# A second buffer for one activation tile in a block of mLSTM, S5 and expert lookup on one Trainium2 core

## The chip, the cores and the metric

The kernel runs on one core of one Trainium2 chip. The metric is the device time of one execution in microseconds (us). Before the change it is 3209.36 us, the median of three runs (3203.93 to 3209.98). A separate execution was recorded by the hardware profiler; every row below comes from that one.

The engines are named as in the profile: PE multiplies matrices (PEld loads its weights), DVE and ACT work on tiles in on-chip memory, POOL and SP here mostly issue DMAs (SPq is SP's DMA queue). Sixteen DMA engines serve all queues.

## What is computed

The reference is one block on 512 tokens of width 2048: a normalisation, a projection, a chunked mLSTM and an S5 scan, an output projection with a residual, and then the part that matters here, a lookup of experts. Each token and each of 8 heads picks 16 of 16384 experts; the activation of an expert is a GELU of the token's dot product with a row of the first table `u_tab`, and it weighs a row of the second table `v_tab`:

```python
def block(args):
    xt, it, gt = args
    ue = jnp.take(u_tab, it, axis=0)
    ve = jnp.take(v_tab, it, axis=0)
    act = jax.nn.gelu(jnp.einsum('td,ted->te', xt, ue).astype(f32), approximate=False)
    return jnp.einsum('te,ted->td', (gt * act).astype(ve.dtype), ve)
```

## The kernel before

The experts are taken in two ways. 72 groups of 128 experts (28 fixed ones, 44 chosen at run time) are computed densely for all 512 tokens; the picks that fall outside these groups, called rare, are gathered row by row.

**The first table's stage** is the loop `for n, (i, q) in enumerate(units)`: 72 groups `i`, each in four quarters `q`, so 288 units. A unit transposes four blocks of the table tile `ur` on PE (L1485), splits them into a high part `uh` on ACT (L1487) and a low part `ul` on DVE (L1495), and makes 12 matmuls of 512 columns (L116 to L118, in the helper `mm3`) into one accumulator. `h_step` issues `u_unit` (the transposes and `uh`) three units ahead and `u_low` (the `ul`) two ahead of the matmuls. After a group's fourth quarter ACT writes the GELU of the accumulator into a tile `hg` (L1507) and SP stores it to `hg_d` (L1508). `hg` has one buffer, so the next group's L1507 waits until this store has landed. `ur` is loaded by SP for the fixed groups and gathered by POOL for the chosen ones (L1053 in `gather`), two groups ahead.

**Beside it** a generator is advanced after each unit, as far as a budget of 3 per unit goes. `gbuild` makes the table of gates: eight chunks of 64 tokens, each built in a tile `Gb` of one buffer. DVE makes one-hot tiles (L1071, L1450), PE multiplies them into a bank `tp` (L1438, three such banks), ACT writes the bank into `Gb` (L1439), and when a chunk is full SP stores it with four DMAs of 1 MB to `gt_d` (L1459) in pieces of 64 numbers. The first L1439 of the next chunk writes into the same tile, so it waits for all four. After a chunk, `HOLD` keeps the table of gates back for eight units:

```python
            for a in range(0, P, 32):
                sp.dma_start(gv[:, a:a + 32, c:c + GC], Gb[:, a:a + 32, :])
            UT["hold"] = UT["step"] + HOLD
```

In these units the budget goes to `rare`: POOL gathers 128 rows of a table into a tile `gr` (L1349, 1 MB, three buffers in this stage), and DVE multiplies and sums each (`junk`, L1346). All stores on SP's queue are issued in the order of the program, so an `hg` store that follows a chunk's four stores goes behind them.

**Memory.** Tiles on the right side of the on-chip memory are `pk` (kept to the end), then `ix` (closed after `flags`), and on it the pools of the stages. `tri` and `oneb` are constants in `pk`; their last readers are matmuls in `select` and `flags`.

After this stage the second table's stage multiplies all groups with `v_tab` in two halves and finishes the rare picks.

Of the kernel before, what the change touches and what calls it, by code (L numbers as in the profile page):

```python
# [8 lines left out]
F32 = mybir.dt.float32  # L9
# [3 lines left out]
BF16 = mybir.dt.bfloat16  # L13
# [6 lines left out]
P = 128  # L20
T = 512
# [27 lines left out]
def hybrid_block(ctx: ExitStack, tc: tile.TileContext, x, norm1_g, w_in, b_gates, conv_w, mnorm_g,  # L49
# [7 lines left out]
    def pool(name, bufs, side="left"):  # L57
        return tc.tile_pool(name=name, bufs=bufs, side=side, reuse_waits="tile")
# [32 lines left out]
    def mm_bank(shape=(P, 512)):  # L91
        return PS["p"].tile(list(shape), F32, name="mm", bufs=PS["mm"])
# [22 lines left out]
    def mm3(o, ah, al, bh, bl, start, stop):  # L115
        pe.matmul(o, ah, bh, start=start, stop=False)  # L116
        pe.matmul(o, ah, bl, start=False, stop=False)  # L117
        pe.matmul(o, al, bh, start=False, stop=stop)  # L118
# [738 lines left out]
    pk = ctx.enter_context(pool(name="pk", bufs=1, side="right"))  # L857
    iotaF = pk.tile([P, P], F32, name="iotaF")
    pcol = pk.tile([P, 1], F32, name="pcol")
    jt = pk.tile([P, P, 2], BF16, name="jt")  # L860
    tri = pk.tile([P, P], BF16, name="tri")
    oneb = pk.tile([P, P], BF16, name="oneb")
    i1b = pk.tile([P, T], BF16, name="i1b")
    i2b = pk.tile([P, T], BF16, name="i2b")
    DT = pk.tile([P, 5, T], BF16, name="DT")
# [7 lines left out]
    ix = ixs.enter_context(pool(name="ix", bufs=1, side="right"))  # L873
    i1T, i2T, gT = (ix.tile([P, T], F32, name=n) for n in ("i1T", "i2T", "gT"))
    subT = ix.tile([P, 2, P], F32, name="subT")

    xn_d = dram.tile([T, D], F32, name="xn_d")
    gt_d = dram.tile([P * P, T], F32, name="gt_d")
# [586 lines left out]
    up = ustk.enter_context(pool(name="up", bufs=1))  # L1465
# [32 lines left out]
    def h_unit(i, q):  # L1498
        if q == 0:
            UT["h", i] = mm_bank()  # L1500
        uh, ul = UT.pop(("u", i, q))
        for a in range(4):
            k = q * 4 + a
            mm3(UT["h", i], uh[:, a, :], ul[:, a, :], xh[:, k, :], xl[:, k, :], k == 0, k == 15)
        if q == 3:
            hg = up.tile([P, T], F32, name="hg")
            s.activation(hg, UT.pop(("h", i)), AF.Gelu)  # L1507
            sp.dma_start(hg_d[i], hg)  # L1508

# [3 lines left out]
    def h_step(i, q):  # L1513
        n = i * 4 + q
        while un[0] < len(units) and un[0] < n + 4:
            u_unit(*units[un[0]])
            un[0] += 1
        while un[1] < len(units) and un[1] < n + 3:
            u_low(*units[un[1]])
            un[1] += 1  # L1520
        h_unit(i, q)
# [197 lines left out]
```

## Time and profile before

| | |
|---|---|
| median of three runs | 3209.36 us |
| the profiled execution, its own time | 3199.87 us |
| its span | 3198.1 us |
| PE, PEld busy | 91%, 77% |
| DVE, ACT, POOL busy | 70%, 31%, 26% |
| mean granted clock of TensorE | 0.956 of full speed |
| DMA | 691.93 MB, 216 GB/s over the span |

Busy time of PE counts overlapping matmuls and is no measure of how near PE is to its peak; it is read here for gaps. The first table's stage goes from about 1055 us (the first `hg`) to 2320 us (the last), and the table of gates is built from about 1500 us to 2190 us. An average over the span says little about it, so the rows below are of single stretches, in us from the start of the span.

### The profile page before, as it was taken

The numbers are of one execution on the slowest core, as the hardware profiler recorded it, in microseconds if no ns is written. First come the engines' busy times: TensorE is split into PE (matmuls) and PEld (weight loads), VectorE is DVE, ScalarE is ACT, GpSimd is POOL, SyncE is SP. The second block draws the span as 40 slices with busy tenths as digits, with TensorE's granted clock in tenths as the row PEclk, the third lists the DMA queues.
The fourth block names the chain that finished last, engine by engine and source line by source line (L and its number), as shares of the span: only waits on it lengthen the run. The fifth ranks groups of instructions, "written<-read, shape, count | busy, mean of one in ns | idle before, by whom it ended". The sixth has DMA issues, their size and how long they took to land. (4 is left out here: it accounts for less than half of the span.)

```text
span 3198.1 us, 45174 instructions
## 1 busy us (share of the span) xinstructions
PE 2921.0 (91%) x17540; PEld 2461.6 (77%) x17540; DVE 2236.1 (70%) x3666; ACT 977.7 (31%) x1491; POOL 839.0 (26%) x656
## 2 busy tenths in 40 slices
PE   7999999999799999998987888787789998999997
PEld 5888978899688887887776776676667776778886
DVE  7467543432388877866866776676687888898875
ACT  5343565432322321121222222222122222332223
POOL 3000111000200000002311232221343888745760
PEclk9999999999899999998998999898899999999998
DMA  4422344344322322634865487877899998999973
GB/s 141 128 86 85 101 117 114 119 161 137 130 86 80 109 85 83 254 136 170 312 232 187 134 280 244 284 247 251 326 379 396 401 342 311 418 406 388 368 291 136
DMA packets 366141, 691.93 MB, mean 216 GB/s; under 512 B 169490, under 2 KB 248850, under 8 KB 320338
## 3 DMA queue, kind: packets, MB, share of 16 engines
q0 software_dynamic: 74240, 393.57, 32.6%
q1 hardware_dynamic: 291680, 295.40, 28.1%
q8 instruction: 140, 2.29, 0.3%
q14 instruction: 81, 0.66, 0.1%
HBM read 644.04 MB, written 96.86 MB: 232 GB/s over the span
## 5 line engine op out<-in xcount | busy, mean ns | idle before, releaser
L116 PE MATMUL mm<-xh,uh 128*128 128x512 f32 x1152 | 494.1, 429 | 0.0
L117 PE MATMUL mm<-xl,uh 128*128 128x512 f32 x1152 | 464.4, 403 | 0.0
L118 PE MATMUL mm<-xh,ul 128*128 128x512 f32 x1152 | 464.0, 403 | 0.0
L1346 DVE SCALAR_TENSOR_TENSOR junk<-gr,xa 128x2048 f32<-128x2048 f32 x147 | 335.9, 2285 | 98.4 <-DMA gr<-in_peer_u_dram,rl 68.6
L113 DVE TENSOR_TENSOR wl<-wr,wh 128x1024 fp32r<-128x1024 f32 (+1 forms) x144 | 187.1, 1302 | 237.8 <-ACT wh L112 237.7
L1353 DVE SCALAR_TENSOR_TENSOR xa<-gr,racts,xa 128x2048 f32<-128x2048 f32 x147 | 345.0, 2347 | 1.1
L1349 POOL DMA_INDIRECT gr<-in_peer_u_dram,rl x147 | 187.6, 1276 | 590.7 <-DVE junk L1346 522.5
L1487 ACT ACTIVATE uh<-tu 128x512 fp32r<-128x512 f32 x288 | 170.8, 598 | 439.4 <-PE tu L1485 431.0
L1349 POOL DMA_INDIRECT gr<-in_peer_v_dram,rl x147 | 251.2, 1709 | 184.8 <-DVE xa L1353 128.7
L116 PE MATMUL mm<-wh,xh 128*128 128x256 f32 (+1 forms) x1024 | 294.7, 288 | 0.0
L118 PE MATMUL mm<-wh,xl 128*128 128x256 f32 (+1 forms) x1024 | 288.9, 282 | 1.7 <-DVE xl L113 1.7
L1495 DVE TENSOR_TENSOR ul<-tu,uh 128x512 fp32r<-128x512 f32 x288 | 196.4, 684 | 132.8 <-ACT uh L1487 96.4
L117 PE MATMUL mm<-wl,xh 128*128 128x256 f32 (+1 forms) x1024 | 289.2, 282 | 0.0
L1485 PE MATMUL tu<-ident,ur 128*128 128x128 f32 x1152 | 183.1, 283 | 112.2 <-DVE ul L1495 111.3
L117 PE MATMUL tp<-vl,ewh 128*128 128x512 f32 x576 | 231.9, 403 | 42.9 <-DVE vl L113 41.3
L118 PE MATMUL mm<-xh,wl 128*128 128x512 f32 x640 | 256.3, 400 | 12.1 <-DVE wl L113 12.1
L118 PEld LDWEIGHTS mm<-xh,ul 128*128 128x128 f32 x1152 | 225.0, 195 | 53.6
L112 ACT ACTIVATE ewh<-hgl 128x512 fp32r<-128x512 f32 x144 | 91.1, 632 | 548.6 <-PE mm L117 255.9
L116 PE MATMUL mm<-xh,wh 128*128 128x512 f32 x640 | 257.8, 403 | 0.0
L116 PEld LDWEIGHTS mm<-xh,uh 128*128 128x128 f32 x1152 | 227.2, 197 | 39.4
L117 PEld LDWEIGHTS mm<-xl,uh 128*128 128x128 f32 x1152 | 227.1, 197 | 39.3
L117 PE MATMUL mm<-xl,wh 128*128 128x512 f32 x640 | 255.2, 399 | 0.0
(498 smaller groups left out, 6036.5 us busy)
## 6 DMA issues: line engine op xcount, KB each, us to landing
wr<-in_w_in_dram SPq DMA_DIRECT2D x80, 512.0 KB
gt_d<-Gb SPq DMA_DIRECT2D x32, 1024.0 KB
ur<-in_peer_u_dram SPq DMA_DIRECT2D x28, 1024.0 KB
vr<-in_peer_v_dram SPq DMA_DIRECT2D x56, 512.0 KB
hg_d<-hg SPq DMA_DIRECT2D x72, 256.0 KB
hgl<-hg_d SPq DMA_DIRECT2D x72, 256.0 KB
w_d<-hgl SPq DMA_DIRECT2D x72, 256.0 KB
hgl<-w_d SPq DMA_DIRECT2D x72, 256.0 KB
```

What stands on the lines that cost most here:

```text
L112: s.activation(hi, src, AF.Copy)
L113: v.tensor_tensor(lo, src, hi.bitcast(F32), op=OP.subtract)
L116: pe.matmul(o, ah, bh, start=start, stop=False)
L117: pe.matmul(o, ah, bl, start=False, stop=False)
L118: pe.matmul(o, al, bh, start=False, stop=stop)
L1346: v.scalar_tensor_tensor(UT["junk"], t, 1.0, xg, op0=OP.mult, op1=OP.mult, accum_out=a)
L1349: g.indirect_dma_start(out=t, out_offset=None, in_=v2 if w else u2, in_offset=IOA(ap=col, axis=0), bounds_check=P * P - 1, oob_is_err=False)
L1353: v.scalar_tensor_tensor(acc, t, a, acc, op0=OP.mult, op1=OP.add)
L1485: pe.transpose(p[:, a, :], ur[:, k * P:(k + 1) * P], ident)
L1487: s.activation(uh, p, AF.Copy)
L1495: v.tensor_tensor(ul, p, uh.bitcast(F32), op=OP.subtract)
```

## The change

`hg` gets two buffers, so that one group's GELU waits for the store of the group before the previous one. Since a second `hg` needs 2 KB more in each partition, the constants `tri` and `oneb` move from the pool that lives to the end into the pool `ix`, which is closed after `flags`, when both have had their last reader.

```diff
@@ -858,8 +858,6 @@
     iotaF = pk.tile([P, P], F32, name="iotaF")
     pcol = pk.tile([P, 1], F32, name="pcol")
     jt = pk.tile([P, P, 2], BF16, name="jt")
-    tri = pk.tile([P, P], BF16, name="tri")
-    oneb = pk.tile([P, P], BF16, name="oneb")
     i1b = pk.tile([P, T], BF16, name="i1b")
@@ -873,6 +871,8 @@
     i1T, i2T, gT = (ix.tile([P, T], F32, name=n) for n in ("i1T", "i2T", "gT"))
     subT = ix.tile([P, 2, P], F32, name="subT")
+    tri = ix.tile([P, P], BF16, name="tri")
+    oneb = ix.tile([P, P], BF16, name="oneb")
@@ -1503,7 +1503,7 @@
         if q == 3:
-            hg = up.tile([P, T], F32, name="hg")
+            hg = up.tile([P, T], F32, name="hg", bufs=2)
             s.activation(hg, UT.pop(("h", i)), AF.Gelu)
             sp.dma_start(hg_d[i], hg)
```

No engine's instructions change their order; what changes is for which DMA an instruction waits. Two places on ACT show it. `DMAHW1` and the like are the semaphores of SP's stores, taken in turn; an ACT row that names four of them is the first write into `Gb` after a chunk's store. First the end of the first chunk, on ACT, before:

```order
L1439 ACTIVATE Gb<-tp 128x128x4 [waits PE_49] x4
L1487 ACTIVATE uh<-tu 128x512 [waits DVE_49,PE_49] x4
L1507 ACTIVATE hg<-mm 128x512 [waits DMAHW2_49,PE_49,Activation_49]
L1487 ACTIVATE uh<-tu 128x512 [waits DVE_49,PE_49] x4
L1507 ACTIVATE hg<-mm 128x512 [waits DMAHW7_49,PE_49,Activation_49]
L1487 ACTIVATE uh<-tu 128x512 [waits DVE_49,PE_49]
L1439 ACTIVATE Gb<-tp 128x128x4 [waits DMAHW5_49,DMAHW4_49,DMAHW6_49,DMAHW3_49,PE_49]
```

and the same place now:

```order
L1439 ACTIVATE Gb<-tp 128x128x4 [waits PE_49] x4
L1487 ACTIVATE uh<-tu 128x512 [waits DVE_49,PE_49] x4
L1507 ACTIVATE hg<-mm 128x512 [waits DMAHW1_49,PE_49]
L1487 ACTIVATE uh<-tu 128x512 [waits DVE_49,PE_49] x4
L1507 ACTIVATE hg<-mm 128x512 [waits DMAHW2_49,PE_49]
L1487 ACTIVATE uh<-tu 128x512 [waits DVE_49,PE_49]
L1439 ACTIVATE Gb<-tp 128x128x4 [waits DMAHW5_49,DMAHW4_49,DMAHW6_49,DMAHW3_49,PE_49]
```

Semaphores 3 to 6 are the chunk's four stores and 7 is the `hg` store right behind them. The second `hg` waited for 7 and now waits for 2, an older store; the write into `Gb` waits for 3 to 6 as before, one `uh` later. Now the end of the second chunk, on ACT, before:

```order
L1507 ACTIVATE hg<-mm 128x512 [waits DMAHW2_49,PE_49,Activation_49]
L1487 ACTIVATE uh<-tu 128x512 [waits DVE_49,PE_49] x4
L1507 ACTIVATE hg<-mm 128x512 [waits DMAHW7_49,PE_49,Activation_49]
L1487 ACTIVATE uh<-tu 128x512 [waits DVE_49,PE_49] x4
L1507 ACTIVATE hg<-mm 128x512 [waits DMAHW0_49,PE_49,Activation_49]
L1439 ACTIVATE Gb<-tp 128x128x4 [waits DMAHW5_49,DMAHW4_49,DMAHW6_49,DMAHW3_49,PE_49]
```

and now:

```order
L1507 ACTIVATE hg<-mm 128x512 [waits DMAHW1_49,PE_49]
L1487 ACTIVATE uh<-tu 128x512 [waits DVE_49,PE_49] x4
L1507 ACTIVATE hg<-mm 128x512 [waits DMAHW2_49,PE_49]
L1487 ACTIVATE uh<-tu 128x512 [waits DVE_49,PE_49] x4
L1507 ACTIVATE hg<-mm 128x512 [waits DMAHW7_49,PE_49]
L1439 ACTIVATE Gb<-tp 128x128x4 [waits DMAHW5_49,DMAHW4_49,DMAHW6_49,DMAHW3_49,PE_49]
```

Here too 7 is the `hg` store behind the chunk. The wait for it has moved by one group, from the second `hg` of the place to the third, four `uh` later; the `Gb` row follows it directly.

## Rows read from the trace of the kernel before

**Rows 1.** Waits of ACT, 1450 to 2330 us: total us, times, longest
```profile
ACT hg L1507 <- DMA hg_d<-hg: 185.5, 7, 32.1
```
**Rows 2.** Waits of PE in the same stretch
```profile
PE tu L1485 <- DVE ul L1495: 110.7, 21, 20.7
PE tp L1438 <- ACT Gb L1439: 35.8, 3, 14.9
```
**Rows 3.** Timeline of SP, second chunk: start, us, queue, line; x is a count
```profile
1654.15 38.38 SPq L1459 DMA_DIRECT2D gt_d<-Gb  x4
1692.62 15.02 SPq L1508 DMA_DIRECT2D hg_d<-hg  x3
```
**Rows 4.** Timeline of ACT, second chunk; in brackets the idle time and its releaser
```profile
1656.14 0.60 ACT L1507 ACTIVATE hg<-mm 128x512 f32<-128x512 f32 x1 [1.53 <-issue]
...
1698.81 0.60 ACT L1507 ACTIVATE hg<-mm 128x512 f32<-128x512 f32 x1 [32.07 <-DMA hg_d<-hg]
```
**Rows 5.** Timeline of PE, second chunk: the transposes that open a unit
```profile
1673.36 0.66 PE L1485 MATMUL tu<-ident,ur 128*128 128x128 f32 x4
1676.61 0.60 PE L1485 MATMUL tu<-ident,ur 128*128 128x128 f32 x4
...
1700.67 1.12 PE L1485 MATMUL tu<-ident,ur 128*128 128x128 f32 x4 [20.73 <-DVE ul L1495]
```
**Rows 6.** Timeline of ACT and PE, first chunk (the fifth and sixth repeat it)
```profile
1614.01 0.60 ACT L1507 ACTIVATE hg<-mm 128x512 f32<-128x512 f32 x1 [25.98 <-DMA hg_d<-hg]
...
1614.98 1.09 ACT L1439 ACTIVATE Gb<-tp 128x512 f32<-128x512 f32 x2
...
1615.64 1.44 PE L1438 MATMUL tp<-go,go 128*128 128x128 bf16 x12 [9.80 <-ACT Gb L1439]
```
**Rows 7.** Windows: us, busy PE, PEld, DVE, ACT, POOL, then clock, DMA share, GB/s
```profile
1680.00:1685.00 5.00, 0.00 (x0) 0.00 (x0) 0.21 (x2) 0.00 (x0) 1.94 (x2) 0.72 1.07 416
...
1690.00:1695.00 5.00, 0.00 (x0) 0.00 (x0) 0.00 (x0) 0.00 (x0) 0.00 (x0) 0.50 1.04 263
```
**Rows 8.** Timeline of POOL, second chunk: the first two gathers after the wait
```profile
1703.09 0.98 POOL L1349 DMA_INDIRECT gr<-in_peer_u_dram,rl  x1 [20.37 <-DVE junk L1346]
1708.72 1.44 POOL L1053 DMA_INDIRECT ur<-in_peer_u_dram,esel  x1 [4.65 <-PE tu L1485]
```
**Rows 9.** Timeline of PE, third chunk: the first unit after its wait, and what follows it
```profile
1787.01 1.12 PE L1485 MATMUL tu<-ident,ur 128*128 128x128 f32 x4 [7.76 <-DVE ul L1495]
...
1792.34 1.55 PE L1438 MATMUL tp<-go,go 128*128 128x128 bf16 x24
```
**Rows 10.** Timeline of ACT and PE, fourth chunk
```profile
1869.62 0.60 ACT L1507 ACTIVATE hg<-mm 128x512 f32<-128x512 f32 x1 [16.83 <-DMA hg_d<-hg]
...
1871.10 0.60 PE L1485 MATMUL tu<-ident,ur 128*128 128x128 f32 x4
```
**Rows 11.** Timeline of ACT and PE, seventh chunk (stored from 2107.30 us)
```profile
2119.94 0.59 ACT L1507 ACTIVATE hg<-mm 128x512 f32<-128x512 f32 x1
...
2143.63 0.60 ACT L1507 ACTIVATE hg<-mm 128x512 f32<-128x512 f32 x1 [2.21 <-PE mm L118]
...
2134.61 1.11 PE L1485 MATMUL tu<-ident,ur 128*128 128x128 f32 x4 [8.73 <-DVE ul L1495]
```
**Rows 12.** Timeline of PE, eighth chunk
```profile
2237.07 1.12 PE L1485 MATMUL tu<-ident,ur 128*128 128x128 f32 x4 [18.57 <-DVE ul L1495]
```
**Rows 13.** Windows of the eighth chunk's end and of the later stages, columns as in 7
```profile
2230.00:2240.00 10.00, 2.93 (x9) 2.55 (x10) 3.64 (x4) 2.66 (x5) 0.51 (x1) 0.50 0.56 149
2240.00:2250.00 10.00, 9.21 (x40) 7.12 (x39) 7.34 (x9) 1.68 (x3) 6.85 (x4) 0.90 0.68 224
...
2250.00:2330.00 80.00, 54.42 (x219) 42.44 (x220) 57.84 (x62) 13.27 (x22) 27.34 (x22) 0.86 0.93 346
2330.00:2600.00 270.00, 243.67 (x1016) 195.84 (x1015) 221.12 (x198) 66.86 (x83) 155.50 (x91) 0.96 1.00 396
...
2800.00:3100.00 300.00, 298.39 (x1313) 246.01 (x1312) 266.36 (x185) 88.64 (x112) 181.16 (x106) 1.00 0.94 368
```

## The prediction

> **What bounds the kernel now.** I first looked for who waits for the `hg` store. In the waits of ACT from 1450 to 2330 us there is one line for it: 185.5 us in 7 waits, the longest 32.1 [rows 1]. That is ACT's loss, not the kernel's. PE does nearly all the work of this stage, so I next read what PE loses there: 110.7 us in 21 waits for `ul` (which needs `uh`, which stands behind the waiting GELU on ACT) and 35.8 us in 3 waits for a bank that ACT empties into `Gb` [rows 2]. So at most 146.5 us of PE's time hang on ACT's lateness, whatever its reason.
>
> Why the store is late is seen on SP's queue. In the second chunk SP begins to issue the four `gt_d` stores at 1654.15, is busy with them for 38.38 us, and only then comes to the `hg` store [rows 3], which holds a GELU of 1656.14. The next GELU begins to wait at 1698.81 - 32.07 = 1666.74 and goes at 1698.81 [rows 4]. PE's own gap there is 20.73 us, ending at 1700.67 [rows 5]; it begins at 1679.94, since PE still had three units in hand. Every chunk of the table of gates but the seventh has such a wait; the other groups have none.
>
> **The second buffer.** It moves the wait, as the order of ACT's instructions shows, from the GELU after a chunk's `hg` to the one after that. It does not make the store land earlier. So each of the eight places is to be priced by itself: how many more units ACT can prepare before it meets the next wait for the same four stores. One unit of PE is 1676.61 - 1673.36 = 3.25 us [rows 5].
>
> *First, fifth and sixth chunk.* One or two `uh` after the waiting GELU comes the first write into `Gb`, and that waits for the four stores themselves. In the first chunk the GELU goes at 1614.01, the write into `Gb` at 1614.98, and PE, which stood for 9.80 us, goes on at 1615.64 [rows 6]. PE was not waiting for `uh` there, but for a bank: it had filled three and the fourth is emptied by just that write. Taking the GELU out of the way leaves the same wait with another name. What is gained is the GELU and one `uh` that then no longer stand between the landing and the write (1614.98 - 1614.01, about 1.0 us) and the part of the landing that belongs to the `hg` store alone, 0.26 MB behind the chunk. The slowest nearby rate is 263 GB/s [rows 7], which makes that 1.0 us. So 2 us a place, 6 us for the three. The bounds are nothing, and 6.5 us a place if the one or two further `uh` did free PE.
>
> *Second chunk.* Eight `uh` stand before the next write into `Gb`. The second GELU now runs at once, and the third waits for what the second waited for. PE gets four units more, 13.0 us, before it is out of work. Against that stands what these units bring with them. The DMA engines are busy for a share of 1.0 and more until the stores have landed, at 416 GB/s while row gathers are among them [rows 7]. The first gathers after the wait are a `gr` and a `ur`, issued by POOL at 1703.09 and 1708.72, after idling for DVE and PE [rows 8]; with the units pulled forward they are issued some 15 us earlier, into the busy stretch. Each is 1.05 MB, at 416 GB/s 2.5 us, so the landing, and PE's resumption with it, comes up to 5 us later. I take the whole of it: 13.0 - 5.0 = 8 us. The bounds are 0 (the gathers push the landing out by all that is gained) and 13.
>
> The Trainium skill (DMA: Bandwidth & Descriptors, Queues, rings and completion order) says that each DMA engine goes round the queues it has work for, a packet at a time. By that rule a gather put in on POOL's queue does take turns with the older store and delays it, which is the value I took; if instead the store's queue went first, this place would give the full 13.
>
> *Third chunk.* PE's gap is 7.76 us, and the first unit after it takes 1792.34 - 1787.01 = 5.33 us [rows 9] against 3.25, because the granted clock has dropped in the gap (in the second chunk's gap it is 0.72, then 0.50, of full speed [rows 7], that is from the 2.4 GHz level to 1.2). Four units, 13.0 us, are longer than the gap, so it goes and the slow unit with it: 7.76 + 2.08 = 9.8, say 10 us. Bounds 0 and 10. In the second chunk a gap of some 8 us stays, so I count no gain from the clock there.
>
> *Fourth chunk.* The GELU waits 16.83 us until 1869.62, but PE starts units without idling at 1871.10 and has work in hand [rows 10]. Nothing; at most 3. *Seventh chunk.* Its GELU does not wait [rows 11]. Nothing.
>
> *Eighth chunk.* PE's gap is 18.57 us [rows 12], and no chunk follows, so again four units, 13 us, come free. But from here on the DMA engines set the pace: a share of 0.93 from 2250 to 2330 us and of 1.00 from 2330 to 2600 [rows 13]. Such a stretch ends earlier only by the DMA time that stood empty before it: (1 - 0.56) x 10 + (1 - 0.68) x 10 = 7.6 us from 2230 to 2250 [rows 13]. With three row tiles for gathers not all of that can be filled; I take 5. Bounds 0 and 13.
>
> *What is moved in memory* costs nothing: no instruction is added, and `tri` and `oneb` have had their last reader before `ix` closes. The next tiles of that memory wait for older readers only, so the cover is not a piece of work but the order itself.
>
> **The sum.** 6 + 8 + 10 + 0 + 0 + 5 = 29 us. What is gained up to 2190 us moves everything behind it forward: the work of the second table's stage is the same, DMA by DMA, and it ends bound by PE (298.39 of 300 us busy [rows 13]). The profiled execution had 3199.87 us for its span of 3198.1, so it would have 3171. It was 9.5 us below the median of the three runs, 3209.36. Against the median I forecast **3180 us**.
>
> **The rivals.**
>
> *All of PE's waiting goes.* That needs the landing to come before the eight units of the hold are through. PE's gaps behind the `hg` waits are 20.73, 7.76 and 18.57 us [rows 5, 9, 12] and the 35.8 us of the three waits for a bank [rows 2], 82.9 us, and with a slow unit of some 2 us behind each of the six near 95: 3114. For it speaks the size of [rows 1]; against it that the write into `Gb` is next in line and waits for the same stores. A sentence in the Trainium skill (Trainium Kernel Development and Optimization, Best Practices) asks for double buffers to overlap DMA with compute, and by it the time would be this one; [rows 6] speak against it. Chance 0.04.
>
> *Nothing is gained, because the DMA engines bound these stretches.* From the start of a chunk's store to its landing they have no free time, so every unit pulled forward brings its gathers in and pushes the landing out: 8 and 5 fall to 0, the three places of 2 us too, and the third chunk's 10 is lost to a gather of the kind the seventh shows. 3209, within 0.2%. For it speaks the share in [rows 7]; against it that only two gathers, 5 us, follow in the 13 us after the second chunk's wait. Chance 0.11.
>
> *It gets slower, by the wait that the seventh chunk shows.* There no GELU waits, yet its next one comes 23.69 us later (2119.94 to 2143.63) where four units make 13.0, and PE stands 8.73 us for `ul` with full DMA queues [rows 11]: the rows that DVE and PE need come late because they share the engines with the store. If the pulled gathers bring that on in the second, third, fourth and eighth chunk, 10.7 us each on top of what is there, it is 43 us lost less the 6 of the other three: 3209 + 37 = 3246. It decides from the point where a needed row lands later than the store itself. Against it: in a chunk where PE stands until the landing anyway, such a wait lies inside that time. Chance 0.05.
>
> *The change doesn't do what it says.* The order on ACT shows the wait moved in every group, so I give this no chance of its own.
>
> **How the numbers follow.** A difference of about 0.2%, 6.4 us, can be told from none. The forecast (some of the 29 us, from 7 to 60) has 0.80; with the first rival faster is 0.84, the same 0.11, slower 0.05. The upper bounds (3 x 6.5 + 13 + 10 + 3 + 13 = 58.5) give 3151 and no gain gives 3209. The range goes from 3151 to 3205; what it leaves out is the first and last rival and most of the second, near 0.2.
>
> **What would show it.** In the profile after, right: the line of ACT's waits for the `hg` store shrinks to some 60 us in three waits or so, each on the third GELU of a chunk; a new line has `Gb` (L1439) waiting for DMA `gt_d`, three or four times, some 20 us each; PE's waits for a bank stay near 35.8 us and those for `ul` fall by 20 to 30; the third chunk has no gap and no slow unit. Wrong: no line of `Gb` waiting for DMA (the first rival), or PE's waits for `ul` unchanged with landings later by what was gained (the second), or new waits of PE or DVE for gathered rows in chunks that had none (the third). The step I trust least is the delay of the landing by pulled gathers.

## The result and the profile after

| | before | after |
|---|---|---|
| median of four runs each | 3209.49 us | 3187.36 us (3178.38 to 3193.81) |
| the profiled execution, its own time | 3199.87 us | 3178.38 us |
| its span | 3198.1 us | 3176.5 us |
| DMA | 691.93 MB | 691.93 MB |

The ratio of the runs is 0.9937, with a 95% interval of 0.9917 to 0.9956: 22 us less by the medians, 21.5 by the profiled executions. The forecast was 29 less, 3180.

The waits of ACT from 1450 to 2330 us, in the kernel after (total us, times, longest), answer to [rows 1]:

```profile
ACT hg L1507 <- DMA hg_d<-hg: 58.7, 3, 32.3
ACT Gb L1439 <- DMA gt_d<-Gb: 57.8, 3, 20.4
```

The seven waits of the GELU for its store, 185.5 us, have become three, and a line that was not there before has come: the first write into `Gb` waits for the chunk's own store. Together they are 116.5 us, so ACT waits 69 us less. PE, in the same stretch, answers to [rows 2]:

```profile
PE tu L1485 <- DVE ul L1495: 80.5, 21, 12.8
PE tp L1438 <- ACT Gb L1439: 42.9, 4, 14.5
```

PE loses 146.5 - (80.5 + 42.9) = 23.1 us less, close to the 21.5 us between the profiled executions. A third of the 69 us that ACT no longer waits, and an eighth of the 185.5 us that stood in its line, were PE's.

Where it came from is seen by following one GELU behind each place through both timelines of ACT (start of L1507, us):

| place | before | after | ahead by | gained there | forecast |
|---|---|---|---|---|---|
| ahead of the first chunk's wait | 1574.49 | 1575.53 | -1.0 | | |
| first chunk | 1622.16 | 1620.77 | 1.4 | 2.4 | 2 |
| second | 1725.10 | 1718.19 | 6.9 | 5.5 | 8 |
| third | 1810.95 | 1793.45 | 17.5 | 10.6 | 10 |
| fourth | 1896.08 | 1879.40 | 16.7 | -0.8 | 0 |
| fifth | 1990.23 | 1971.12 | 19.1 | 2.4 | 2 |
| sixth | 2089.74 | 2067.68 | 22.1 | 3.0 | 2 |
| seventh | 2159.21 | 2136.88 | 22.3 | 0.2 | 0 |
| eighth, by the last GELU | 2319.27 | 2294.68 | 24.6 | 2.3 | 5 |
| end of the span | 3198.1 | 3176.5 | 21.6 | -3.0 | 0 |

In a second profile of the changed kernel, that of the last experiment, the same GELUs against the same profile of the kernel before give 2.7, 5.0, 10.1, -0.6, -0.2, 2.5, 0.5 and 2.6 for the eight places. The second, third and eighth place repeat; a single place of 2 us, as the fifth, is no more than the difference between two profiles of one kernel.

The first chunk, on ACT's and PE's timelines of the kernel after (start, us, engine, line; in brackets the idle time and its releaser), answers to [rows 6]:

```profile
1592.86 0.60 ACT L1507 ACTIVATE hg<-mm 128x512 f32<-128x512 f32 x1 [2.17 <-PE mm L118]
...
1614.33 1.08 ACT L1439 ACTIVATE Gb<-tp 128x512 f32<-128x512 f32 x2 [20.38 <-DMA gt_d<-Gb]
...
1614.97 1.44 PE L1438 MATMUL tp<-go,go 128*128 128x128 bf16 x12 [9.04 <-ACT Gb L1439]
```

The GELU that had to wait until 1614.01 goes 21 us sooner. It helps PE by next to nothing: the same bank frees PE at 1614.97 where it did at 1615.64, 1.7 us of gain with the 1.0 that the changed kernel was behind. The wait stands under another name.

The second chunk, on the timelines of SP, ACT, POOL and PE, answers to [rows 3 to 5, 8]:

```profile
1652.18 43.17 SPq L1459 DMA_DIRECT2D gt_d<-Gb  x4
...
1667.58 0.60 ACT L1507 ACTIVATE hg<-mm 128x512 f32<-128x512 f32 x1 [2.17 <-PE mm L118]
...
1701.62 0.60 ACT L1507 ACTIVATE hg<-mm 128x512 f32<-128x512 f32 x1 [20.76 <-DMA hg_d<-hg]
...
1682.83 0.99 POOL L1349 DMA_INDIRECT gr<-in_peer_u_dram,rl  x1 [0.30 <-issue]
1685.10 1.20 POOL L1053 DMA_INDIRECT ur<-in_peer_u_dram,esel  x1 [1.29 <-PE tu L1485]
1721.27 0.99 POOL L1349 DMA_INDIRECT gr<-in_peer_u_dram,rl  x1 [34.97 <-DVE junk L1346]
...
1679.56 0.66 PE L1485 MATMUL tu<-ident,ur 128*128 128x128 f32 x4 [1.74 <-DVE ul L1495]
...
1684.23 0.60 PE L1485 MATMUL tu<-ident,ur 128*128 128x128 f32 x4
...
1702.76 1.44 PE L1438 MATMUL tp<-go,go 128*128 128x128 bf16 x12 [14.46 <-ACT Gb L1439]
```

The second GELU runs at once and the third waits, as the order on ACT had it. The two gathers that came after the wait now come ahead of the landing, and no other. From the start of the chunk's store to the GELU that waits for it there are 1698.81 - 1654.15 = 44.7 us before and 1701.62 - 1652.18 = 49.4 us after: the two gathers have pushed the landing out by 4.8 us.

### The profile page after: what moved, and what is told of

It is laid out like the page before. It is cut to its first block, busy times and chain, and to the rows that moved or that the text cites. A ratio compares the mean times of both kernels' runs of the same rounds, so it can differ in the third digit from the quotient of the medians.

```text
span 3176.5 us, 45172 instructions
## 1 busy us (share of the span) xinstructions
PE 2914.3 (92%) x17540; PEld 2455.5 (77%) x17540; DVE 2236.1 (70%) x3666; ACT 979.1 (31%) x1491; POOL 846.7 (27%) x656
## 2 busy tenths in 40 slices
DMA packets 366141, 691.93 MB, mean 218 GB/s; under 512 B 169490, under 2 KB 248850, under 8 KB 320338
## 3 DMA queue, kind: packets, MB, share of 16 engines
q1 hardware_dynamic: 291680, 295.40, 28.4%
## 5 line engine op out<-in xcount | busy, mean ns | idle before, releaser
L112 ACT ACTIVATE wh<-wr 128x1024 fp32r<-128x1024 f32 (+1 forms) x144 | 166.9, 1162 | 260.8 <-PE mm L118 103.8
```

The lines of the kernel that those rows point to most:

```text
L112: s.activation(hi, src, AF.Copy)
```

## The experiments

Each is timed beside the kernel before on the same chip, and what counts is the ratio to it; chips differ between groups of experiments, so medians of different groups are not set side by side. The first words of each say which kernel its edit starts from.

**Only the memory moves.** The changed kernel with one buffer.

```diff
-            hg = up.tile([P, T], F32, name="hg", bufs=2)
+            hg = up.tile([P, T], F32, name="hg")
```

> Only the two constants move, the activation tile keeps one buffer. Theory (the whole gain comes from the wait for the store that moves by one group): no difference from the kernel before, within 0.2%, and the 185 us of ACT's waits for the hg store are there again in seven waits. Rival (the addresses of the tiles changed the time): 10 us or more below the kernel before.

Ratio 1.0014 (1.0004 to 1.0023), 188.7 us of waits for the `hg` store in seven waits. The move of `tri` and `oneb` gains nothing; by the ratio it costs some 4 us (1 to 7), within the 0.2% that was expected.

**A longer hold.** The changed kernel.

```diff
-HOLD = 8
+HOLD = 11
```

> The changed kernel with the table of gates held back for 11 units instead of 8 after each chunk. Theory (from a chunk's store to its landing the DMA engines are the bound, because every unit of the hold brings its row gathers): three more units take 9.75 us of PE but bring some 3.6 row gathers and part of a table tile, 10 to 11 us of DMA, into the same stretch, so the landing moves out by about as much; the waits of Gb and hg for the stores, 116 us in the changed kernel, shrink by less than 30 us and the time is 3175 to 3195. Rival (the hold is merely too short for a landing that stays where it is): each of the three Gb waits and the two long hg waits shrinks by nearly 10 us, 40 us or more in all, and the time falls to 3150 or less.

Ratio 0.9954 (0.9937 to 0.9970), 3187.98 us: the same as the changed kernel within the intervals. ACT's waits for stores in the profile:

```profile
ACT hg L1507 <- DMA hg_d<-hg: 99.9, 6, 29.7
```

They were 116.5 us in the changed kernel, 17 us more than here. With three more units between a chunk and the next write into `Gb`, that write no longer waits, but the GELU ahead of it does. The 40 us or more that the expectation gives to a fixed landing are too many, since a longer hold does not move the third GELU, which has the two long waits. So the landing is better read by itself. In the first chunk

```profile
1558.95 35.06 SPq L1459 DMA_DIRECT2D gt_d<-Gb  x4
...
1621.18 0.60 ACT L1507 ACTIVATE hg<-mm 128x512 f32<-128x512 f32 x1 [16.09 <-DMA hg_d<-hg]
```

there are 62.2 us from the chunk's start to the end of the wait (about 1 us of it, by the prediction's estimate, for the `hg` store right behind the chunk's), where the changed kernel has 51.0 (1563.33 to 1614.33); in the fifth 54.4 and not 47.8, in the sixth 56.8 and not 50.8. In these three the landing moves out with the work that is let in, by 6 to 11 us; in the second, third and eighth, where the third GELU waited before too, it changes by -7.2, 1.7 and -2.1.

**One buffer, and a queue of its own for the store.** The kernel before; ACT issues the store.

```diff
-            sp.dma_start(hg_d[i], hg)
+            s.dma_start(hg_d[i], hg)
```

> The kernel before, one buffer, but the hg store is issued by ACT on a queue of its own and not by SP behind the chunk's stores. Theory (the wait is for the place on SP's queue, and behind it stands the wait of Gb for the chunk itself): ACT's waits for the hg store fall from 185 us to under 30, the waits of Gb for gt_d appear, 60 to 110 us in four to six places, and the time is that of the changed kernel or up to 8 us below it, 3175 to 3190. Rival (the store is late because the DMA engines are full, on whatever queue it stands): the hg waits stay over 90 us and the time stays within 0.2% of the kernel before.

Ratio 0.9945 (0.9929 to 0.9962), 3186.67 us. The lines of ACT's waits for DMAs:

```profile
ACT Gb L1439 <- DMA gt_d<-Gb: 89.0, 5, 20.9
ACT uh L1487 <- DMA gt<-gt_d: 26.0, 1, 26.0
```

The GELU has no wait for its store left, with one buffer. So the store was late for its place on SP's queue, not because the DMA engines were full: beside them, on another queue, it lands in time. And the time is that of the changed kernel, because `Gb` waits for the chunk in five places. Either change takes away the same wait and meets the same second one. The 26 us in the last line are a cost of this variant alone: near the end of the stage the `hg` store on ACT has to wait for a semaphore that SP's loads for the next stage use too, and ACT stands behind it. 24 of the 72 `hg` stores on ACT have such a wait ahead of them; from 1450 to 2330 us only this one held ACT up.

**No row gathers in the hold.** The changed kernel. The rows are summed later, in the units of the table of gates, behind the last chunk, or in the second table's stage.

```diff
-            c = c or (pump1("g") if n0 is not None else 0)
+            c = c or (pump1("g") if n0 is not None and n >= UT["hold"] else 0)
```

> The changed kernel, but no row gather and no sum of a row is done in the eight units of the hold; they come later in the stage, or in the second table's stage. Theory (row gathers push the landing out): a chunk's store, 17 to 20 us of DMA when alone, lands within the 26 us of the hold, so the waits of Gb and hg for stores fall from 116 us to under 15, and the table-of-gates part of the stage gets 25 to 50 us shorter; the rows that are left over make the second table's stage longer by 2.5 us of DMA each, so the total may come out on either side. Rival (the store itself is what takes 40 us and the gathers only fill its pauses): the waits for stores stay above 60 us.

Ratio 0.9942 (0.9925 to 0.9958), 3182.07 us, the same time as the changed kernel, by another way. ACT has no wait for the stores of `Gb` or `hg` from 1450 to 2330 us, and PE's waits for `ul` in that stretch are

```profile
PE tu L1485 <- DVE ul L1495: 22.0, 4, 11.3
```

in place of 80.5, and none for a bank. How a chunk's store goes without gathers is seen in windows behind its start at 1562.22 us (columns as in [rows 7]):

```profile
1565.00:1570.00 5.00, 5.00 (x26) 4.17 (x25) 1.26 (x2) 1.20 (x2) 0.00 (x0) 1.00 1.18 354
1570.00:1575.00 5.00, 5.00 (x28) 4.12 (x27) 1.22 (x2) 1.19 (x3) 0.00 (x0) 1.00 1.24 290
1575.00:1580.00 5.00, 5.00 (x26) 4.08 (x25) 0.85 (x2) 1.10 (x3) 0.94 (x1) 1.00 1.17 282
1580.00:1585.00 5.00, 5.00 (x28) 4.12 (x26) 1.57 (x3) 1.10 (x2) 0.00 (x0) 1.00 1.07 271
1585.00:1590.00 5.00, 5.00 (x25) 4.13 (x24) 3.51 (x6) 1.19 (x3) 1.75 (x2) 1.00 0.42 138
```

PE is busy throughout at the full clock, and the DMA engines are done some 25 us after the start, inside the hold (17 to 20 were expected for the store alone; table tiles go beside it). In the changed kernel's first chunk there are 51 us, from 1563.33 on SP to the write into `Gb` at 1614.33. The last GELU comes at 2167.6 us and not at 2294.7, so the first table's stage is 127 us shorter; the eighth chunk is stored at 2073.05 us and not at 2168.19, 95 us earlier where 25 to 50 were expected. The second stage is longer by nearly as much as the first is shorter: 1007 us from the last GELU to the end of the span where the changed kernel takes 882. The rows tell why (sums of rows of the first table, two instructions each, behind the last GELU; the last two columns are DMA share and GB/s, and an instruction across the edge of a window stands in both):

```profile
2167.00:2295.00 128.00, 66.56 (x59) 0.88 0.98 383
2295.00:2320.00 25.00, 13.27 (x13) 0.93 1.02 420
2320.00:2600.00 280.00, 115.53 (x102) 0.92 0.98 390
```

Counted once these are 170 instructions, 85 rows, where the changed kernel has 42 instructions, 21 rows, left at that point. With 64 rows more the second stage is 125 us longer, 2.0 us each, and the DMA engines are at 0.98 and more there.

**The same with one buffer.** The edit of the last experiment on the kernel before.

> The kernel before, one buffer, with no row gather in the eight units of the hold. Theory (what makes the store late is the gathers beside it, and a store that lands some 20 us after it begins asks for no second buffer): ACT's waits for the hg store fall from 185 us to under 25, PE has no gap over 5 us at them, and the time is within 6 us of that of the changed kernel without these gathers, 3174 to 3190. Rival (the second buffer is what matters, whatever the gathers do): over 90 us of hg waits stay and the time is within 0.2% of the kernel before.

Ratio 0.9943 (0.9925 to 0.9961): the same as with two buffers. There are more waits left than expected,

```profile
ACT hg L1507 <- DMA hg_d<-hg: 49.3, 7, 12.0
```

but PE, which is some three units ahead, loses 25.8 us for `ul` against 22.0, and from 1555 to 2120 us only 3.6 in two waits. Once the store lands some 25 us after it begins, the second buffer has next to nothing left to win.

**Rows in the last three units of the hold, and a larger budget.** Three versions of the changed kernel: rows allowed in the hold's last three units; no rows in the hold but a budget of 3.6 for a unit; rows in the last three units and that budget.

```diff
-            c = c or (pump1("g") if n0 is not None else 0)
+            c = c or (pump1("g") if n0 is not None and n >= UT["hold"] - 3 else 0)
```
```diff
-UBUD = 3.0
+UBUD = 3.6
```

> The changed kernel; in the hold the row gathers are allowed again in its last three units only, when most of the chunk has landed. Theory: waits for stores stay under 30 us in all, some 25 more rows than without gathers in the hold are done in the first table's stage, each takes 2.5 us of DMA out of the second, and the time is 3160 to 3178, below the changed kernel by 10 us or more. Rival (the time is set by the sum of work on DVE or DMA over both stages, wherever the rows are done): 3180 to 3190, as the changed kernel.

> The changed kernel with no row gather in the hold and a budget of 3.6 per unit in place of 3.0, so that each chunk is built in fewer units and more rows follow in the units behind the last chunk. Theory: no waits for stores, more rows done in the first table's stage than without the larger budget, units of the stage bound by DVE where rows are done; 3160 to 3180. Rival (the sum of work sets the time): 3180 to 3190.

> Both: row gathers in the last three units of the hold, and a budget of 3.6. Theory: waits for stores under 40 us, the most rows in the first table's stage of the three, 3155 to 3178. Rival (the sum of work sets the time): 3180 to 3190.

Ratios 0.9856 (0.9819 to 0.9892), 0.9878 (0.9849 to 0.9907) and 0.9866 (0.9829 to 0.9902); medians 3156.57, 3162.55 and 3160.04 us. All three beat the changed kernel, with intervals that do not reach its own, and cannot be told from each other. The first expectation held but for the waits, under 30 us expected:

```profile
ACT Gb L1439 <- DMA gt_d<-Gb: 30.3, 2, 15.4
ACT hg L1507 <- DMA hg_d<-hg: 16.5, 1, 16.5
```

The second was to have none and has 39.5 us in seven waits. The third has 73.0 us of waits for `gt_d`, where all waits were to stay under 40, and is no slower; it has 24 instructions of the first table's row sums left behind 2320 us, 12 rows, where the first has 60, 30 rows. The rival, that the sum of the work sets the time wherever it is done, falls with all three.

**Between, without the second buffer, and the change again.** Rows in the last three units with one buffer; rows in the last five with two; the changed kernel itself.

> The kernel before, one buffer, with row gathers in the last three units of the hold only. Theory (with few gathers beside the store it lands soon after the next group's GELU is due, so the second buffer is worth the few waits that are left): hg waits of 50 to 90 us against 30 us of Gb and 17 us of hg waits with two buffers, and 5 to 15 us above the two-buffer version, 3160 to 3175. Rival (the second buffer is what makes the gathers' place count): within 0.3% of the changed kernel, 3178 to 3195.

> The changed kernel with row gathers in the last five units of the hold, between all eight (the changed kernel) and three. Theory: each unit more brings its 1.2 gathers before the landing, so the waits for stores lie between the 47 us of three units and the 116 us of eight, 60 to 100 us, and the time lies between the two, 3160 to 3180. Rival (three was a lucky place in the program): no order, above the changed kernel or below three units.

> The changed kernel itself, to stand beside the other two on the same chip. Theory: 0.992 to 0.996 of the kernel before, as in its first comparison, with ACT's waits for gt_d and hg stores at 100 to 130 us in some six places. Rival (its gain is by chance of the first chip): 0.998 or more.

Ratios 0.9906 (0.9889 to 0.9924), 0.9891 (0.9874 to 0.9907) and 0.9934 (0.9909 to 0.9959). The changed kernel repeats its first ratio, 0.9937. Five units lie between three and eight, with 63.8 + 29.1 = 93 us of waits, as expected; by the ratio five and three cannot be told apart. One buffer with three units has 91.3 us of waits for the `hg` store, just over the 50 to 90 expected, in place of 47 with two, and is 0.5% above the two-buffer version by the ratios (0.9906 and 0.9856). That step is not settled: the intervals touch at 0.9889 and 0.9892, and in the profiled executions PE loses as much for `ul` and banks with one buffer (38.1 + 11.1 = 49.2 us) as with two (25.6 + 26.9 = 52.5). The rival, that the second buffer is what makes the place count, asked for 3178 us or more; the median is 3168.30. With one buffer the place of the gathers alone is thus worth about as much as the second buffer alone (0.9937 and 0.9934), or more; the intervals overlap.

## Why the prediction was right

*The wait moves and does not go.* Shown: in the first, fifth and sixth chunk the write into `Gb` waits, 57.8 us in three waits; in the second, third and eighth the third GELU, 58.7 us in three. The text said some 60 us in three for the GELU and some 20 each in three or four for `Gb`. The queue of its own shows the two waits apart. PE's waits for `ul` fell by 30.2 us, where 20 to 30 were named; those for a bank were to stay near 35.8 and are 42.9, because the three old ones fell to 28.4 and the second chunk's gap came under this name, with 14.46.

*First, fifth and sixth chunk, 2 us each.* They gave 2.4, 2.4 and 3.0, in the second profile 2.7, -0.2 and 2.5.

*Second chunk, 13 - 5 = 8 us.* The push of the landing was sized at 5.0 and measured 4.8. But 5.5 came, not 8: PE got two of the four units, which start at 1679.56 and 1684.23 us. Then stands a matmul that needs a bank, and the bank needs the write into `Gb`. PE's gap there is 14.46 us. (The text speaks of a gap of some 8 us that stays; by its own sum 20.73 - 8 = 12.7 stay, since the 5 us of the push belong to it.) By the Trainium skill (DMA: Bandwidth & Descriptors, Queues, rings and completion order) each DMA engine goes round the queues that it has work for; the 4.8 us agree with that, since two later gathers delayed an older store by about their own 5.0 us.

*Third chunk, 10 us.* It gave 10.6. PE's gap of 7.76 us and the slow unit [rows 9] are both gone, as PE's timeline in the kernel after shows, where bank matmuls and units come in turn and none of the rows, those left out included, has idle time ahead of it:

```profile
1774.87 1.55 PE L1438 MATMUL tp<-go,go 128*128 128x128 bf16 x24
1776.26 0.61 PE L1485 MATMUL tu<-ident,ur 128*128 128x128 f32 x4
...
1779.47 1.55 PE L1438 MATMUL tp<-go,go 128*128 128x128 bf16 x24
1780.86 0.60 PE L1485 MATMUL tu<-ident,ur 128*128 128x128 f32 x4
```

*Fourth and seventh, nothing.* -0.8 and 0.2.

*Eighth chunk, 5 us, the other term that was mis-sized.* It gave 2.3. The text let the four free units fill most of 7.6 us of empty DMA time behind the landing [rows 13]. They did not. In the kernel after, the windows before and behind the eighth landing at 2229 us (columns as in [rows 7]) read

```profile
2220.00:2230.00 10.00, 0.00 (x0) 0.00 (x0) 0.00 (x0) 0.75 (x2) 0.00 (x0) 0.64 0.81 322
2230.00:2240.00 10.00, 8.88 (x32) 7.28 (x33) 8.61 (x9) 3.00 (x6) 4.38 (x3) 0.68 0.30 91
```

that is (1 - 0.81) x 10 + (1 - 0.30) x 10 = 8.9 us empty. The four units brought their gathers in ahead of the landing and moved it out: from the store's start to the waiting GELU there are 2229.25 - 2168.19 = 61.1 us, before 2235.20 - 2190.47 = 44.7, 16 us more. The rows are, of the kernel after and then of the one before:

```profile
2168.19 42.57 SPq L1459 DMA_DIRECT2D gt_d<-Gb  x4
2229.25 0.60 ACT L1507 ACTIVATE hg<-mm 128x512 f32<-128x512 f32 x1 [32.32 <-DMA hg_d<-hg]
...
2190.47 38.49 SPq L1459 DMA_DIRECT2D gt_d<-Gb  x4
2235.20 0.60 ACT L1507 ACTIVATE hg<-mm 128x512 f32<-128x512 f32 x1 [31.30 <-DMA hg_d<-hg]
```

PE even gets a gap ahead of the landing, for a sum that waits for its row, and a second one at the landing. Together they are 19.7 us, where one of 18.57 stood before [rows 12]:

```profile
2199.07 2.29 DVE L1346 SCALAR_TENSOR_TENSOR junk<-gr,xa 128x2048 f32<-128x2048 f32 x1 [3.48 <-DMA gr<-in_peer_u_dram,rl]
...
2204.19 2.29 DVE L1346 SCALAR_TENSOR_TENSOR junk<-gr,xa 128x2048 f32<-128x2048 f32 x1 [2.83 <-DMA gr<-in_peer_u_dram,rl]
...
2207.15 1.11 PE L1485 MATMUL tu<-ident,ur 128*128 128x128 f32 x4 [8.08 <-DVE ul L1495]
...
2231.11 1.12 PE L1485 MATMUL tu<-ident,ur 128*128 128x128 f32 x4 [11.62 <-DVE ul L1495]
```

This is the mechanism of the second and third rival, and here it took back all that was free at the landing; the 2.3 us come behind it.

*What is moved in memory.* The text put it at nothing. The first experiment has 1.0014 for it alone, so if the two add up, the second buffer by itself is worth some 4 us more than the change. No row here shows where the 4 us go.

*Passing through to the end.* 24.6 us were gained by the last GELU and 21.6 are left at the end. The loss stands where the second stage begins. Its first matmul waits for ACT's split of a tile of `v_tab`, before and after:

```profile
PE tp L116 <- ACT vh L112: 7.0, 1, 7.0
...
PE tp L116 <- ACT vh L112: 10.8, 1, 10.8
```

It starts at 2326.21 us before and at 2305.48 after, 20.7 ahead. The kernel in which only the memory moves has 9.9 us there, with one buffer. What the second stage adds is not settled: the lead goes from 20.7 to 21.6 in this profile and from 16.6 to 13.3 in the second one, and runs of one kernel lie up to 15 us apart.

*The rivals.* That all of PE's waiting goes fell with the line of `Gb`. That nothing is gained fell as a whole, but its mechanism is what limits the gain: take the gathers out of the hold of the changed kernel and the waits for stores are gone. That it gets slower did not come.

## What to carry to other kernels

A second buffer behind a late store buys the time until the next wait for the same landing, no more; look down the waiting engine's order for that wait before counting the first one's length. Ask why the landing is late: here a queue of its own for the small store, or work that keeps off the DMA engines while the large store drains, did as much with one buffer (0.9945 and 0.9943), and the place of the gathers together with the buffer gave twice what the buffer gave alone (ratios 0.9856 and 0.9937). And what an engine is allowed to do sooner brings its DMAs along.

## What was not expected of the hardware

While a chunk's store of 4.2 MB in pieces of 256 bytes drained without row gathers beside it, all DMA engines were busy for some 25 us and moved 271 to 290 GB/s from 1570 to 1585 us, table tiles included; windows with row gathers in them reach 416 to 420. In a window of 5 us the share of the DMA engines read up to 1.24, so it is not a strict share. And a store on ACT's queue was held for 26 us by a semaphore that loads on SP's queue use as well. That comes from the way this program takes its semaphores in turn: a queue of one's own is not free of the others.
